# Decode rows of a hybrid layer spread over all 128 partitions, with the array used in four tiles

## The chip, the cores and the metric

One core of a Trainium2 chip runs one layer of a decoder trunk. The metric is the device time of one execution in microseconds. Of the engines, TensorE multiplies and transposes (PE in the profile, PEld its weight loads), VectorE (DVE) and ScalarE (ACT) work element by element and empty PSUM, GpSimd (POOL) prepares weight sums, and SyncE (SP) issues most transfers.

## The reference, cut to what matters

A layer mixes 1024 tokens of one prompt and 64 decode tokens (8 sequences of 8 tokens) with two groups of four heads of 128 columns, and then runs a convolutional feed-forward block. The retention heads work in chunks; the decode sequences are one chunk of 8 rows each with a state that is given:

```python
scores = jnp.einsum('bhnd,bhmd->bhnm', qc, kc) * dmat[None]
out = (jnp.einsum('bhnm,bhmv->bhnv', scores, vc)
       + jnp.einsum('bhnd,bhdv->bhnv', qc, S) * xi[None, :, :, None])
S_new = (S * chunk_decay[None, :, None, None]
         + jnp.einsum('bhmd,bhmv->bhdv', kc * zeta[None, :, :, None], vc))
```

Here `dmat` holds gamma to the power of the distance below the diagonal. An mLSTM head has the same three parts (own values, state, update) with weights `w` made of running gate sums, and a normaliser that rides along as a 129th column of the state. Each head's output is normalised per row and gated.

## The kernel before, in words

All tensors lie with features on partitions and tokens on columns: `q`, `k`, `v` of a head are 128 x 1088, 1024 prompt columns and then 64 decode columns. Projections run in split fp32 (three products per weight tile, `product`, L160) over four blocks of 272 columns.

`mix_head` handles one head. `front` (L571 on) takes one or two chunks of 128 columns, or the 64 decode columns as "chunk 8": it transposes k and v (L577, L578) into PSUM, scales k into `kz` and v into `vt`, for an mLSTM head broadcasts the gate rows over the partitions (L595, L597), adds the mask (L601) and takes the exponential (L603), then forms the scores (L618) and masks them into `pt` (L620). A retention head has a mask of its own with its decay in it, 128 columns for the prompt and 64 for the decode rows.

`pair_of` finishes two prompt chunks: update products (L706), own values (L711), the state product (L713), the state itself (L717, L719), and `stats`. `sample` finishes the decode rows, which lie on 64 partitions: q is laid out so that each sequence's 8 columns stand alone among 64 (`qx`, L665); one product of the own values (L667) and eight with the eight states (L669) add up in one PSUM tile of 64 rows. The values are then masked into eight copies, one for each sequence (`vx`, L674), and update products of three or four states each (L682) are added to the states on VectorE (L685 or L687). `finish` normalises rows, transposes them back (L655) and writes them to `yT` (L659, L661).

The order within a head is chunks 0 and 1, 2 and 3, the decode rows, 4 and 5, 6 and 7, each `front` written one step ahead, and each `finish` one step behind. The order of instructions on each engine is set by a planner, which follows the program's order as priority and a model of the times: it puts projection products of the next head between the small products. Small products and their results use six PSUM banks (`psB`), projections two (`psA`). GpSimd meanwhile prepares sums of feed-forward weights (L754).

Of the kernel before, what the change touches and what calls it, by code (L numbers as in the profile page):

```python
# [16 lines left out]
P = 128  # L17
D = 1024
KT = D // P
LP = 1024  # L20
# [25 lines left out]
C_ID, C_BLK, C_RM, C_RMS = 0, 128, 136, 136 + 512  # L46
C_ZE, C_XI, C_XI2 = C_RMS + 256, C_RMS + 264, C_RMS + 300
C_N = C_XI2 + 36
X_NEG, X_NEGS, X_SEL = 0, 128, 192
X_N = 192 + 1024  # L50


def _tables():
# [3 lines left out]
    s = np.arange(TS)  # L57
    up = i[:, None] <= i[None, :]
    same = s[:, None] // LS == s[None, :] // LS
    ups = same & (s[:, None] <= s[None, :])  # L60
    for h in range(NH):
        lg = LG[h]
        c[:, C_RM + h * P:C_RM + (h + 1) * P] = np.where(up, SCALE * np.exp(-(i[:, None] + 1) * lg), 0.0)
        c[:TS, C_RMS + h * TS:C_RMS + (h + 1) * TS] = np.where(
            ups, SCALE * np.exp(-(s[:, None] % LS + 1) * lg), 0.0)
        c[:, C_ZE + h] = SCALE * np.exp((CH - 1 - i) * lg)
        c[:TS, C_ZE + NH + h] = SCALE * np.exp((LS - 1 - s % LS) * lg)
        xi = np.ones((P, 9))
        xi[:, :8] = np.exp((i + 1) * lg)[:, None]
        xi[:TS, 8] = np.exp((s % LS + 1) * lg)  # L70
        c[:, C_XI + h * 9:C_XI + h * 9 + 9] = xi
        c[:, C_XI2 + h * 9:C_XI2 + h * 9 + 9] = xi * xi
    c[:TS, C_BLK:C_BLK + NB] = s[:, None] // LS == np.arange(NB)[None, :]
    x = np.zeros((P, X_N), np.float64)
    x[:, X_NEG:X_NEG + P] = np.where(up, 0.0, NEG)
    x[:, X_NEGS:X_NEGS + TS] = NEG
    x[:TS, X_NEGS:X_NEGS + TS] = np.where(ups, 0.0, NEG)
# [15 lines left out]
def hybrid_layer_kernel(ctx: ExitStack, tc: tile.TileContext, a: dict, o: dict):  # L93
# [211 lines left out]

    def token_norms():
        ps = bank(psB, 9, "rcol")
        for c in range(9):
            m = CH if c < 8 else TS
            nc.tensor.matmul(ps[:m, c:c + 1], rb[:, c * CH:c * CH + m], ident[:, 0:1], start=True, stop=True)  # L310
        nc.vector.tensor_copy(rcol[:, :8], ps[:, :8])
        nc.vector.tensor_copy(rcol[:TS, 8:9], ps[:TS, 8:9])
# [5 lines left out]
    negsb = mp.tile([P, TS], BF16, name="negsb")  # L318
# [28 lines left out]
    def gate_consts():  # L347
# [8 lines left out]
        nc.vector.tensor_copy(negsb, xst[:, X_NEGS:X_NEGS + TS])  # L356
# [16 lines left out]
    def gate_rows():  # L373
# [64 lines left out]
        for g in range(0, 9, 3):  # L438
            ps = bank(psB, 288, f"cols{g}").rearrange("p (i c) -> p i c", i=3)
            for i in range(3):  # L440
                c = g + i
                n = CH if c < 8 else TS
                nc.tensor.transpose(ps[:n, i, :68], stk[:, c * CH:c * CH + n], ident[:68, :68])
                nc.vector.tensor_copy(cols[:n, c, :].rearrange("p (j r) -> p j r", j=3),
                                      ps[:n, i, :].rearrange("p (j r) -> p j r", j=3)[:, :, :NH])
# [44 lines left out]

    def csl(c):
        return slice(c * CH, c * CH + (CH if c < 8 else TS))

    def rows_of(c):
        return CH if c < 8 else TS
# [29 lines left out]
    def mix_head(hd, ml):  # L525
# [44 lines left out]

        def front(cs):  # L571

            c0, L, n = cs[0], len(cs), rows_of(cs[0])
            nmc = f"{nm}{c0}"
            px = bank(psB, 512, f"x_{nmc}").rearrange("p (j i n) -> p j i n", j=2, i=2)
            for i, c in enumerate(cs):
                nc.tensor.transpose(px[:n, 0, i, :], k[:, csl(c)], ident)  # L577
                nc.tensor.transpose(px[:n, 1, i, :], v[:, csl(c)], ident)  # L578
            kz = m2.tile([P, 2, P], F32, tag="kz", name=f"kz_{nmc}")
            if ml:  # L580
                nc.vector.tensor_tensor(kz[:n, :L], px[:n, 0, :L, :],
                                        cols[:n, c0:c0 + L, NH + hd].unsqueeze(2).broadcast_to([n, L, P]), ALU.mult)
            else:
                zc = C_ZE + hd + (0 if c0 < 8 else NH)
                nc.vector.tensor_scalar(kz[:n, :L], px[:n, 0, :L, :], rc(zc, 1, n), None, ALU.mult)
            vt = vts[0]
            vts.append(vts.pop(0))
            for i, c in enumerate(cs):
                nc.scalar.activation(vt[:n, i, :P], px[:n, 1, i, :], AF.Copy, scale=rcol[:n, c:c + 1])
            qs = None  # L590
            if ml:
                pb = bank(psB, 512, f"w_{nmc}").rearrange("p (j i n) -> p j i n", j=2, i=2)
                cs_ = slice(c0 * CH, c0 * CH + L * n)
                flat2 = lambda j: pb[:, j].rearrange("p i n -> p (i n)")[:, :L * n]
                ins = nc.tensor.matmul(flat2(1), sel[:, 1, hd, :], uihl[:, cs_], start=True, stop=True)  # L595
                with tc.issue_after(ins.ins):
                    nc.tensor.matmul(flat2(0), sel[:, 0, hd, :], uihl[:, cs_], start=True, stop=False)  # L597
                wt, qs = (wq[:, turns["wq"] % 2, i].rearrange("p (i n) -> p i n", i=2) for i in range(2))
                turns["wq"] += 1
                for i, c in enumerate(cs):  # L600
                    nc.tensor.matmul(pb[:, 0, i, :n], idb, negb if c < 8 else negsb, start=False, stop=i == L - 1)  # L601
                for i, c in enumerate(cs):
                    nc.scalar.activation(wt[:n, i, :n], pb[:n, 0, i, :n], AF.Exp,  # L603
                                         bias=cols[:n, c, 2 * NH + hd:2 * NH + hd + 1])
                if c0 < 8:
                    nc.vector.tensor_copy(dec[:, c0:c0 + L], pb[:, 1, :, n - 1])
                else:
                    nc.vector.tensor_copy(dec[:, 8:16],
                                          flat2(1).rearrange("p (s l) -> p s l", s=NB)[:, :, LS - 1])
                qv = q[:, c0 * CH:c0 * CH + L * n].rearrange("p (i n) -> p i n", i=L)  # L610
# [827 lines left out]
```

## Time and profile before

| | us |
|---|---|
| median of 3 runs (1367.94 to 1368.15) | 1368.1 |
| span of the profiled execution | 1367.5 |
| that execution's time around its span, from the median | 0.6 |
| TensorE busy | 1345.5 |
| VectorE busy | 1005.6 |
| ScalarE busy | 594.3 |
| GpSimd busy | 428.2 |

The profile's times are microseconds from the start of the span. A matmul's length in it includes its way through the array, so neighbouring rows overlap; the difference of two starts is what an instruction costs. Rows that merge several instructions give the first start and the time to the last end. The retention heads run from 117 to 300 us, the mLSTM heads from 297 to 518 us.

### The profile page before, as it was taken

Reading aid. Unit: us, or ns where it says so; the run is one execution under the profiler, and the core shown is the slowest. Engines: PE = TensorE matmul, PEld = TensorE weight load, DVE = VectorE, ACT = ScalarE, POOL = GpSimd, SP = SyncE. Lnnn points to the kernel's source line nnn. Section 1 sums busy time; section 2 is a strip of 40 time slices with the busy share of each in tenths; the row PEclk is TensorE's granted clock in tenths of the full one; section 3 lists DMA queues with packets and bytes.
Section 4 is the critical chain, followed back from the end, with each engine's and each line's share of the span. In section 5 each row is a group of like instructions: output and inputs, shape, how many; then the busy total and the mean of one; then the engine's idle time right before and its main releaser. Section 6 shows DMA issues by size and latency. Waiting matters only on the chain.

```text
span 1367.5 us, 26897 instructions
## 1 busy us (share of the span) xinstructions
PE 1345.5 (98%) x10583; PEld 1321.4 (97%) x10583; DVE 1005.6 (74%) x2009; ACT 594.3 (43%) x1107; POOL 428.2 (31%) x565
## 2 busy tenths in 40 slices
PE   9999999999999999999989999999999999999996
PEld 9999999999999999999989999999999999999995
DVE  6878875556475366668799978778777788996667
ACT  7544333212222335546364434434334355454562
POOL 0354440579665000000143222221222205872002
PEclk9999999999999999999999999999999999999998
DMA  6434541477885111533124444443444359533363
GB/s 244 143 109 135 172 137 56 146 218 188 223 169 191 49 49 42 183 99 105 57 93 140 155 148 135 134 134 118 143 150 136 126 163 332 176 106 92 95 217 131
DMA packets 92734, 192.80 MB, mean 141 GB/s; under 512 B 16192, under 2 KB 41280, under 8 KB 92096
## 3 DMA queue, kind: packets, MB, share of 16 engines
q1 hardware_dynamic: 80304, 149.03, 33.3%
q0 software_dynamic: 12160, 41.95, 10.7%
q8 instruction: 83, 1.36, 0.4%
q14 instruction: 43, 0.35, 0.1%
q10 hardware_dynamic: 144, 0.11, 0.0%
HBM read 134.58 MB, written 56.47 MB: 140 GB/s over the span
## 4 chain that ended last, share of the span: by engine, by line
PE 92%; DVE 5%; issue 1%; ACT 1%; DMA 1%; SPq 0%; DVEq 0%
PE in L160 27%; PE out L160 6%; PE up_S L1046 6%; PE up_S L1044 6%; PE up_S L1045 6%; PE dn L1255 5%; PE dn L1257 5%; PE dn L1256 5%; PE up_A L1045 4%; PE up_A L1044 4%; PE up_A L1046 4%; PE up_A L1091 1%; PE up_A L1092 1%; PE up_A L1090 1%; PE s_m L618 1%
## 5 line engine op out<-in xcount | busy, mean ns | idle before, releaser
L160 PE MATMUL in<-hh,wh_in 128*128 128x272 f32 x1024 | 298.6, 294 | 1.5 <-ACT wh_in L144 1.5
L160 PE MATMUL in<-hh,wl_in 128*128 128x272 f32 x1024 | 296.4, 291 | 0.0
L160 PE MATMUL in<-hl,wh_in 128*128 128x272 f32 x1024 | 295.6, 291 | 0.0
L160 PEld LDWEIGHTS in<-hh,wh_in 128*128 128x128 f32 x1024 | 192.2, 188 | 4.6 <-issue 2.0
L160 PEld LDWEIGHTS in<-hh,wl_in 128*128 128x128 f32 x1024 | 192.4, 189 | 3.7 <-issue 3.5
L160 PEld LDWEIGHTS in<-hl,wh_in 128*128 128x128 f32 x1024 | 191.9, 188 | 1.7 <-issue 1.5
L144 ACT ACTIVATE wh_up<-st_up 128x1024 fp32r<-128x1024 f32 x84 | 80.4, 959 | 164.9 <-PE up_S L1045 100.5
L146 DVE TENSOR_TENSOR wl_up<-st_up,wh_up 128x1024 fp32r<-128x1024 f32 x84 | 96.5, 1151 | 9.3 <-ACT wh_up L144 9.3
L1184 DVE TENSOR_TENSOR rb<-rb 128x544 fp32r<-128x544 f32 x78 | 75.9, 979 | 36.5 <-ACT rb L1183 35.9
L1018 DVE TENSOR_TENSOR Uv<-Uv,up_S 128x272 f32<-128x272 f32 (+1 forms) x200 | 66.4, 376 | 45.5 <-PE up_S L1046 45.5
L754 POOL TENSOR_TENSOR tab<-tab 128x256 f32<-128x256 f32 x104 | 81.1, 790 | 13.7 <-DMA tab<-in_wu 9.3
L1183 ACT ACTIVATE rb<-rb 128x544 fp32r<-128x544 f32 x78 | 50.4, 650 | 77.1 <-DMA rb<-bd 61.8
L1204 POOL TENSOR_TENSOR wd<-wd 128x512 f32<-128x512 f32 x44 | 71.8, 1657 | 35.0 <-DMA wd<-in_wd 14.4
L1076 POOL TENSOR_TENSOR act<-act 128x544 f32<-128x544 f32 x40 | 64.7, 1618 | 55.2 <-DMA bd<-act 37.4
L1059 DVE SCALAR_TENSOR_TENSOR c<-Uv,vec,c 128x1024 f32<-128x1024 f32 (+1 forms) x88 | 69.0, 789 | 9.0 <-ACT c L1057 9.0
L1009 POOL MEMSET Ug<- 128x2 f32 x22 | 2.2, 99 | 227.7 <-DMA xr<-in_x 117.8
L1059 DVE SCALAR_TENSOR_TENSOR c<-Ug,vec,c 128x1024 f32<-128x1024 f32 x88 | 69.2, 825 | 0.6 <-ACT c L1057 0.6
L754 POOL TENSOR_TENSOR wq<-wq 128x256 f32<-128x256 f32 x56 | 51.0, 920 | 44.8 <-DMA wq<-in_wu 42.6
L754 POOL DMA_DIRECT2D tab<-in_wu x52 | 36.7, 713 | 67.4 <-DVE k_r L486 48.8
L1057 ACT ACTIVATE c<-Ug,vec 128x1024 f32<-128x1024 f32 (+1 forms) x44 | 34.6, 833 | 52.2 <-DVE Ug L1022 46.7
L1044 PE MATMUL up_S<-B3h,wh_up 128*128 128x272 f32 x160 | 47.4, 296 | 3.7 <-ACT Uv L1029 3.7
L146 DVE TENSOR_TENSOR wl_in<-st_in,wh_in 128x1024 fp32r<-128x1024 f32 (+2 forms) x33 | 40.8, 1236 | 13.3 <-ACT wh_in L144 13.3
(544 smaller groups left out, 4642.4 us busy)
## 6 DMA issues: line engine op xcount, KB each, us to landing
rb<-bd SPq DMA_DIRECT2D x76, 272.0 KB, 2.9
st_up<-sd SPq DMA_DIRECT2D x40, 512.0 KB, 3.9
bd<-act SPq DMA_DIRECT2D x33, 544.0 KB, 3.6
st_in<-in_wi SPq DMA_DIRECT2D x31, 512.0 KB, 4.2
tab<-in_wu POOLq DMA_DIRECT2D x52, 256.0 KB, 5.1
sd<-tab POOLq DMA_DIRECT2D x26, 512.0 KB, 3.6
st_up<-in_wu SPq DMA_DIRECT2D x24, 512.0 KB, 3.4
wd<-in_wd SPq DMA_DIRECT2D x44, 256.0 KB, 5.3
```

The source lines that it names most:

```text
L144: act = nc.scalar.activation(hi, x, AF.Copy)
L146: last["split"] = act, eng.tensor_tensor(lo, x, hi.bitcast(F32), ALU.subtract)
L160: nc.tensor.matmul(ps, u[:, k * P:(k + 1) * P], x[b // 2][k // 4][v][:, k % 4, qcols(b)], start=k == term == 0, stop=k == KT - 1 and term ...
L754: last["sums"] = f(*args)
L1044: nc.tensor.matmul(ps, wh[:, c], xh[:, k, n], start=k == 0, stop=False)
L1045: nc.tensor.matmul(ps, wh[:, c], xl[:, k, n], start=False, stop=False)
L1046: nc.tensor.matmul(ps, wl[:, c], xh[:, k, n], start=False, stop=k == 3)
L1059: nc.vector.scalar_tensor_tensor(c, u(i), cw(i), c, ALU.mult, ALU.add)
L1184: nc.vector.tensor_tensor(lo, x, hi.bitcast(F32), ALU.subtract)
L1204: nc.gpsimd.tensor_tensor(quad(p, out), quad(p, x), quad(p, y), op)
L1255: nc.tensor.matmul(t, wh[:, ms], ah, start=k == 0, stop=False)
L1256: nc.tensor.matmul(t, wh[:, ms], al, start=False, stop=False)
```

## The change

The 64 decode columns are spread: four groups of 32, of which the last 16 hold two sequences and the first 16 are the columns ahead of them (16 of the preceding data, masked out). So chunk 8 has 128 columns and its transposes 128 rows, like every other chunk. A view with overlapping windows gives q; k and v are copied by ScalarE into a tile of their own, since they are weights of the array. The state products write 32 partitions each, four groups side by side, and the updates contract 32 partitions each, four groups below one another. The eight masked copies of the values become two (first or second sequence of a group), and the updates four products of two states. The update products stand ahead of `stats`, in four banks taken together. The retention masks become one for the prompt and one for the decode rows; the head's decay comes in as a factor per row (`C_RS`) in a three-operand instruction. Tables and helpers follow (the tables' new layout is cut below).

```diff
+    c[:, C_RM:C_RM + P] = up
+    c[:, C_RMS:C_RMS + P] = ups
...
+        c[:, C_RS + h] = SCALE * np.exp(-(i + 1) * lg)
+        c[:, C_RS + NH + h] = SCALE * np.exp(-(s % LS + 1) * lg)
...
+    def chunk(t, c):
+
+        if c < NCH:
+            return t[:, c * CH:(c + 1) * CH]
+        v = t[:, LP - LEAD:]
+        return bass.AP(v.tensor, v.offset, [list(v.ap[0]), [TS // G, G], [1, GW]])
+
+    def spread(t):
+        return t.rearrange("p (g r) -> p g r", g=G)
+
+    def spread_copy(t, out):
+
+        nc.scalar.activation(spread(out), chunk(t, NCH), AF.Copy)
+        return out
+
+    def spread_tile(name):
+        return m2.tile([P, NB * 129], F32, tag="vx", bufs=1, name=name)
...
-    qx = mp.tile([P, NB * (TS + LS)], F32, name="qx")
+    qx = mp.tile([P, G, 2, GW + LS], F32, name="qx")
     nc.gpsimd.memset(qx, 0.0)
-    qown = qx.rearrange("p (s t) -> p s t", s=NB)[:, :, :LS]
+    qown = qx[:, :, :, LEAD:LEAD + LS]
+    qone = lambda g, e: qx[:, g].rearrange("p e r -> p (e r)")[:, GW * e:GW * (e + 1)]
...
+            if c0 < 8:
+                kc, vc = ([chunk(t, c) for c in cs] for t in (k, v))
+            else:
+                own.append(spread_tile(f"sp_{nm}"))
+                kc, vc = ([spread_copy(t, own[0][:, i * P:(i + 1) * P])] for i, t in enumerate((k, v)))
             for i, c in enumerate(cs):
-                nc.tensor.transpose(px[:n, 0, i, :], k[:, csl(c)], ident)
-                nc.tensor.transpose(px[:n, 1, i, :], v[:, csl(c)], ident)
+                nc.tensor.transpose(px[:, 0, i, :], kc[i], ident)
+                nc.tensor.transpose(px[:, 1, i, :], vc[i], ident)
...
             for i, c in enumerate(cs):
-                nc.tensor.matmul(ps[:, i, :], k[:, csl(c)], q[:, csl(c)], start=True, stop=True)
+                o_ = ps[:, i, :]
+                nc.tensor.matmul(o_ if c < 8 else spread(o_), kc[i], chunk(q, c), start=True, stop=True)
             pt = m2.tile([P, 2, P], F32, tag="pt", name=f"pt_{nmc}")
-            nc.vector.tensor_tensor(pt[:n, :L, :n], ps, mk, ALU.mult)
+            if ml:
+                nc.vector.tensor_tensor(pt[:, :L, :], ps, wt[:, :L, :], ALU.mult)
+            else:
+                m = rc(C_RM if c0 < 8 else C_RMS, P).unsqueeze(1).broadcast_to([P, L, P])
+                nc.vector.scalar_tensor_tensor(pt[:, :L, :], ps, rc(C_RS + hd + (0 if c0 < 8 else NH), 1), m,
+                                               ALU.mult, ALU.mult)
...
         def sample(kz, vt, qs, pt):
-            qv = qs[:, 0, :TS] if ml else q[:, LP:]
-            nc.vector.tensor_copy(qown, qv.rearrange("p (s l) -> p s l", s=NB))
-            po = bank(psB, W, f"o_{nm}8", rows=TS)
-            nc.tensor.matmul(po, pt[:TS, 0, :TS], vt[:TS, 0, :W], start=True, stop=False)
-            for i in range(NB):
-                nc.tensor.matmul(po, qx[:, i * TS:(i + 1) * TS], sb[:, i, :W], start=False, stop=i == NB - 1)
+            qv = spread(qs[:, 0, :])[:, :, LEAD:] if ml else spread(q[:, LP:])
+            nc.vector.tensor_copy(qown, qv.rearrange("p g (e t) -> p g e t", e=2))
+            po = bank(psB, W, f"o_{nm}8")
+            nc.tensor.matmul(po, pt[:, 0, :], vt[:, 0, :W], start=True, stop=False)
+            for e in range(2):
+                for g in range(G):
+                    nc.tensor.matmul(po[GW * g:GW * (g + 1), :], qone(g, e), sb[:, 2 * g + e, :W],
+                                     start=False, stop=e == 1)
...
-            stats(on, po.unsqueeze(1), 0, 1, TS, mv, f"{nm}s")
-            vx = m2.tile([TS, NB, 129], F32, tag="vx", bufs=1, name=f"vx_{nm}")[:, :, :W]
-            nc.vector.tensor_tensor(vx, vt[:TS, 0, :W].unsqueeze(1).broadcast_to([TS, NB, W]),
-                                    cst[:TS, C_BLK:C_BLK + NB].unsqueeze(2).broadcast_to([TS, NB, W]), ALU.mult)
+            vx = own[0][:, 2 * P:2 * P + 2 * W].rearrange("p (e v) -> p e v", e=2)
+            nc.vector.tensor_tensor(vx, vt[:, 0, :W].unsqueeze(1).broadcast_to([P, 2, W]),
+                                    cst[:, C_BLK:C_BLK + 2].unsqueeze(2).broadcast_to([P, 2, W]), ALU.mult)
+            ups = [bank(psB, 2 * W, f"us_{nm}{g}") for g in range(G)]
+            for g, up in enumerate(ups):
+                rows_ = slice(GW * g, GW * (g + 1))
+                nc.tensor.matmul(up, kz[rows_, 0, :], vx[rows_], start=True, stop=True)
+            stats(on, po.unsqueeze(1), 0, 1, mv, f"{nm}s")
             if ml:
                 nc.vector.tensor_tensor(sb, sb, dec[:, 8:16].unsqueeze(2).broadcast_to([P, NB, W]), ALU.mult)
-            step = 3 if ml else 4
-            for j in range(0, NB, step):
-                m = min(step, NB - j)
-                up = bank(psB, m * W, f"us_{nm}{j}").rearrange("p (s v) -> p s v", s=m)
-                nc.tensor.matmul(up, kz[:TS, 0, :], vx[:, j:j + m, :], start=True, stop=True)
-                sj = sb[:, j:j + m, :W]
+            for g, up in enumerate(ups):
+                up = up.rearrange("p (s v) -> p s v", s=2)
+                sj = sb[:, 2 * g:2 * g + 2, :W]
```

## Rows read from the trace of the kernel before

**Rows 1.** The page's first part: busy time, share of the span and instructions of each engine.

```profile
PE 1345.5 (98%) x10583; PEld 1321.4 (97%) x10583; DVE 1005.6 (74%) x2009; ACT 594.3 (43%) x1107; POOL 428.2 (31%) x565
```

**Rows 2.** The chain of waits that ended last, shares of the span by engine.

```profile
PE 92%; DVE 5%; issue 1%; ACT 1%; DMA 1%; SPq 0%; DVEq 0%
```

**Rows 3.** TensorE's waits between 50 and 540 us, the whole answer: engine, tile and line, who was waited for, us in total, times, longest.

```profile
PE yt_m L655 <- DVE on_m L653: 0.4, 1, 0.4
```

**Rows 4.** Busy time of each engine by stage: the last row of the answer, the sum over 120 to 510 us and the mean of its eight stretches, in us.

```profile
sum 390.00, PE 389.38 PEld 369.59 DVE 234.42 ACT 122.31 POOL 178.71; mean PE 48.67 PEld 46.20 DVE 29.30 ACT 15.29 POOL 22.34
```

**Rows 5.** TensorE's timeline over the decode rows of retention head 2: start us, length us, engine, line, operation, what it writes from what, rows and columns of the array, form, count of instructions merged.

```profile
219.82 0.61 PE L618 MATMUL s_r<-q_r,k_r 128*128 128x128 f32 x4
220.36 0.43 PE L667 MATMUL o_r<-vts,pt_r 64*64 64x128 f32 x2
220.72 1.97 PE L669 MATMUL o_r<-sb_r,qx 128*64 128x128 f32 x16
222.61 1.98 PE L682 MATMUL us_r<-vx_r,kz_r 64*128 64x512 f32 x4
224.52 0.39 PE L160 MATMUL in<-hh,wh_in 128*128 128x272 f32 x1
224.75 0.29 PE L160 MATMUL in<-hh,wl_in 128*128 128x272 f32 x1
224.88 0.28 PE L160 MATMUL in<-hl,wh_in 128*128 128x272 f32 x1
```

**Rows 6.** The same view from 222.28 us on, where the row takes only the last four instructions of L669.

```profile
222.08 0.60 PE L669 MATMUL o_r<-sb_r,qx 128*64 128x128 f32 x4
```

**Rows 7.** The weight loads of TensorE beside them.

```profile
220.71 1.73 PEld L669 LDWEIGHTS o_r<-sb_r,qx 128*64 128x64 f32 x16 [0.17 <-issue]
...
223.15 0.19 PEld L682 LDWEIGHTS us_r<-vx_r,kz_r 64*128 64x128 f32 x1 [0.24 <-issue]
223.58 0.19 PEld L682 LDWEIGHTS us_r<-vx_r,kz_r 64*128 64x128 f32 x1 [0.24 <-issue]
```

**Rows 8.** TensorE's timeline where the decode rows of the same head are transposed and scored (the scores, two instructions of L618, stand between the first two rows).

```profile
215.89 0.27 PE L578 MATMUL x_r<-cst,v_r 128*64 128x128 f32 x1
...
216.35 0.71 PE L706 MATMUL u_r<-vts,kz_r 128*128 128x128 f32 x4
216.90 0.39 PE L711 MATMUL o_r<-vts,pt_r 128*128 128x128 f32 x2
```

**Rows 9.** TensorE's timeline where the decode output of the same head is transposed.

```profile
230.50 0.39 PE L713 MATMUL o_r<-S_r,q_r 128*128 128x128 f32 x2
230.72 0.39 PE L711 MATMUL o_r<-vts,pt_r 128*128 128x128 f32 x2
231.04 0.27 PE L655 MATMUL yt_r2s<-cst,on_r2s 64*128 64x64 f32 x1
231.24 0.39 PE L160 MATMUL in<-hh,wl_in 128*128 128x272 f32 x1
231.47 0.29 PE L160 MATMUL in<-hl,wh_in 128*128 128x272 f32 x1
```

**Rows 10.** TensorE's timeline over the decode rows of mLSTM head 2.

```profile
433.57 0.43 PE L667 MATMUL o_m<-vts,pt_m 64*64 64x129 f32 x2
433.93 0.39 PE L160 MATMUL in<-hh,wh_in 128*128 128x272 f32 x1
434.16 0.38 PE L713 MATMUL o_m<-S_m,wq 128*128 128x129 f32 x2
434.47 1.99 PE L669 MATMUL o_m<-sb_m,qx 128*64 128x129 f32 x16
436.39 0.91 PE L682 MATMUL us_m<-vx_m,kz_m 64*128 64x387 f32 x2
437.23 0.39 PE L160 MATMUL in<-hh,wl_in 128*128 128x272 f32 x1
...
437.80 1.35 PE L682 MATMUL us_m<-vx_m,kz_m 64*128 64x387 f32 x4
439.08 0.39 PE L160 MATMUL in<-hh,wl_in 128*128 128x272 f32 x1
```

**Rows 11.** VectorE's normalising of the prompt chunks and TensorE's first transpose of them, in mLSTM heads 0 (two rows) and 2 (two rows).

```profile
332.40 3.17 DVE L653 TENSOR_SCALAR on_m<-on_m,mv_m,A_m 128x128 f32<-128x128 f32 x4
...
334.42 0.27 PE L655 MATMUL yt_m<-cst,on_m 128*128 128x128 f32 x1
...
441.02 1.12 DVE L653 TENSOR_SCALAR on_m<-on_m,mv_m,A_m 128x128 f32<-128x128 f32 x4
...
444.36 0.27 PE L655 MATMUL yt_m<-cst,on_m 128*128 128x128 f32 x1
```

**Rows 12.** Groups by form: line, engine, operation, what it writes from what, count: shortest/median/longest ns, first and last start, forms. The last row is a timeline row of ScalarE: the last piece of v of retention head 2.

```profile
L674 DVE TENSOR_TENSOR vx_r<-vts,cst x4: 1209/1210/1514, 132.0 to 269.1; 64x1024 f32<-64x1024 f32 x4
...
L687 DVE SCALAR_TENSOR_TENSOR sb_r<-sb_r,us_r x8: 660/688/690, 140.2 to 276.8; 128x512 f32<-128x512 f32 x8
...
L620 DVE TENSOR_TENSOR pt_r<-s_r,tab x20: 205/410/425, 121.1 to 282.1; 128x256 f32<-128x256 f32 x16, 64x64 f32<-64x64 f32 x4
...
L624 ACT ACTIVATE on_r2s<-o_r x1: 270/270/270, 222.7 to 222.7; 64x128 f32<-64x128 f32 x1
...
210.88 0.40 ACT L471 ACTIVATE v_r<-in 128x272 f32<-128x272 f32 x1 [2.61 <-PE in L160]
```

More of the change, by code (lines that the diff above doesn't have):

```diff
@@ L304, in pre_norm @@
             nc.vector.tensor_tensor(rot[i][:, o0:o0 + n], rot[i][:, o0:o0 + n], rb[:, o0:o0 + n], ALU.mult)
+    def chunk(t, c):
[10 more added lines that the diff above has]
+        return m2.tile([P, NB * 129], F32, tag="vx", bufs=1, name=name)
     def token_norms():
         ps = bank(psB, 9, "rcol")
+        rs = spread_copy(rb, spread_tile("sp_rb")[:, :P])
         for c in range(9):
[L309 to L312, printed above, removed]
+            nc.tensor.matmul(ps[:, c:c + 1], chunk(rb, c) if c < 8 else rs, ident[:, 0:1], start=True, stop=True)
+        nc.vector.tensor_copy(rcol, ps)
     idb = mp.tile([P, P], BF16, name="idb")
@@ L441, in gate_rows @@
                 c = g + i
[L442 to L445, printed above, removed]
+                x = chunk(stk, c) if c < 8 else spread_copy(stk, spread_tile("sp_stk")[:68, :P])
+                nc.tensor.transpose(ps[:, i, :68], x, ident[:68, :68])
+                nc.vector.tensor_copy(cols[:, c, :].rearrange("p (j r) -> p j r", j=3),
+                                      ps[:, i, :].rearrange("p (j r) -> p j r", j=3)[:, :, :NH])
     yT = []
@@ L489, in evac_rot @@
         return f
[L491 to L495, printed above, removed]
     def early_gate(hid):
@@ L616, in front @@
-            ps = bank(psB, 2 * P, f"s_{nmc}").rearrange("p (i n) -> p i n", i=2)[:n, :L, :n]
-            for i, c in enumerate(cs):
-                nc.tensor.matmul(ps[:, i, :], k[:, csl(c)], q[:, csl(c)], start=True, stop=True)
-            pt = m2.tile([P, 2, P], F32, tag="pt", name=f"pt_{nmc}")
-            nc.vector.tensor_tensor(pt[:n, :L, :n], ps, mk, ALU.mult)
+                    nc.vector.tensor_copy(dec[:, c0:c0 + L], pb[:, 1, :, P - 1])
+                    qv = q[:, c0 * CH:(c0 + L) * CH].rearrange("p (i n) -> p i n", i=L)
@@ L635, in finish @@
+            small = lambda tag: m2.tile([P, 4], F32, tag=tag, name=f"{tag}_{name}")[:, :L]
             vv, A = small("vv"), small("A")
@@ L650, in finish @@
             nc.vector.tensor_tensor(A, A, rd, ALU.mult)
-            ps = bank(psB, L * n, f"yt_{name}")
+            ps = bank(psB, L * P, f"yt_{name}")
             for i in range(L):
-                nc.vector.tensor_scalar(on[:n, i, :P], on[:n, i, :P], mv[:n, i, 0:1], A[:, i:i + 1],
+                nc.vector.tensor_scalar(on[:, i, :P], on[:, i, :P], mv[:, i, 0:1], A[:, i:i + 1],
                                         ALU.subtract, ALU.mult)
-                nc.tensor.transpose(ps[:, i * n:(i + 1) * n], on[:n, i, :P], ident[:n, :n])
-            y = yT[hid // 2][:, hid % 2, c0 * CH:c0 * CH + L * n]
+                nc.tensor.transpose(ps[:, i * P:(i + 1) * P], on[:, i, :P], ident)
+            y = yT[hid // 2][:, hid % 2, c0 * CH:c0 * CH + L * P if c0 < 8 else T]
+            if c0 == 8:
+                ps, y = spread(ps)[:, :, LEAD:], spread(y)
             gain = vec[:, V_HEAD + hid:V_HEAD + hid + 1]
@@ L712, in pair_of @@
                     if c:
-                        prev = nc.tensor.matmul(po[:, i, :], qs[:, i, :] if ml else q[:, csl(c)], S,
+                        prev = nc.tensor.matmul(po[:, i, :], qs[:, i, :] if ml else chunk(q, c), S,
                                                 start=False, stop=True)
```

98 lines of the change are left out of this document (49 added, 49 removed).

## The prediction

> **What bounds the kernel now.** I read the page's busy shares first, then the chain of waits, then what TensorE waited for in the stage that the change touches, then that stage instruction by instruction. TensorE is busy for 98% of the span and the chain that ended last is TensorE for 92% [rows 1, 2]. Busy time alone says little, since its matmuls overlap. The stronger sign is the list of TensorE's waits from 50 to 540 us, all of the projections and heads: one wait, 0.4 us [rows 3]. The planner fills every gap of a head with projection matmuls of the next one, which follow each other every 0.125 us [rows 5]. In 390 us of that stage VectorE works 234 us and ScalarE 122 us [rows 4]. So a microsecond of TensorE issue time taken out of a head is a microsecond of the span, as long as nothing that TensorE waits for is just in time. The other engines' changes count only there.
>
> **What TensorE pays today for the decode rows of one head.** I take retention head 2, where nothing else lies between. An fp32 matmul stands in the trace as two matmul instructions with a weight load each. Full-array instructions over 128 columns follow each other every 0.11 us: two of them fill 230.50 to 230.72 [rows 9]. The own scores end at 219.82 + 4 x 0.11 = 220.26. The projection is back in step at 224.75 - 0.125 = 224.63 [rows 5]. That is 4.37 us for the product with the own values (L667), eight state products (L669) and two updates (L682).
>
> Changing the shape of the array costs extra there. The last four instructions of L669 begin at 222.08, so the next of that kind would begin at 222.52; L682 begins at 222.61, 0.09 later [rows 6]. Then the first instruction of the new shape has its weight load uncovered: L682's first step is 223.15 - 222.61 = 0.54 where the next is 223.58 - 223.15 = 0.43 [rows 6, 7], and the first projection step after it is 0.23 where 0.125 is usual [rows 5]. So a change costs 0.09 plus 0.11 with 128 weight columns. For 32 columns I estimate 0.03, a quarter of 0.11.
>
> **The change, part by part, on TensorE.**
> *Outputs and updates.* After it the own product is full shape (2 x 0.11 = 0.22); then into column tiles (0.09 + 0.03), 16 instructions over 128 columns (X), into row tiles (0.09 + 0.11), 8 instructions over 256 columns (Y), and out (0.09 + 0.11): 0.74 + X + Y. A 256-column step is half of 0.43, 0.215. The trace of before holds no two tiles side by side, so X and Y are bounded. Without any overlap X = 16 x 0.11 = 1.76 and Y = 8 x 0.215 = 1.72: 4.22 us, 0.15 saved. With all four tiles abreast X is four steps and three weight loads (0.53) and Y two steps and three loads (0.43 + 0.11): 1.81 us, 2.56 saved. I take a value between. The code issues tile after tile, and a tile's two instructions follow each other; the second must wait for its own first, and what is queued behind it waits too, if matmuls begin in order. Then only the second of one tile overlaps the first of the next: X = 9 x 0.11 = 0.99, Y = 5 x 0.215 = 1.08: 2.81 us, 1.56 saved.
>
> The Trainium skill (TensorE: Matmul & The Clock Gate, "The mechanism") says that a weight load overlaps a running matmul only if the row group differs; column tiles share all rows, which would speak against X. In L669 the 16 weight loads already lie beside the matmuls of the same rows, at steps of 0.11 (16 in 1.73 us) [rows 7], so the trace does not bear it out; by the rule X would be above 1.76 and the updates alone would gain.
>
> *Shapes that go.* The decode scores were 64 columns wide: from the transpose at 215.89 to the product at 216.90 is 1.01 us; in full shape it is 0.11 + 2 x 0.11 + 4 x 0.11 = 0.77, with the doubled columns in it: 0.24 saved [rows 8]. The transpose of the decode output had 64 rows: 230.72 to 231.47 is 0.75; in full shape 0.22 + 0.11 + 0.125 = 0.46: 0.29 saved [rows 9]. The mLSTM row broadcasts and mask gain 64 columns each, at most 3 x 0.03 = 0.09 per head; I leave it out. So a retention head saves 1.56 + 0.53 = 2.1 us (0.7 to 3.1).
>
> *mLSTM heads.* In head 2 the same work runs from 433.48 (0.09 before L667) to 439.08 + 0.105, 5.7 us, with four projection instructions (0.5) and L713 (0.22) in between: 4.98, since the work there is cut and each cut pays two changes of shape [rows 10]. Against 2.81 that is 2.17 + 0.53 = 2.7; one cut that stays costs 0.4, so I take 2.4 for heads 2 and 3 (1.3 without overlap).
>
> In heads 0 and 1 a wait takes over. VectorE normalises the four prompt chunks from 332.40 to 335.57 and TensorE's transposes of them begin at 334.42, in the middle of it; in head 2 they end at 442.14 and are read from 444.36 [rows 11]. An earlier TensorE only waits there, while what VectorE does before (scaling and adding the states) moves up by what the outputs gain, 0.77 and a little. I take 1.0 each (0 to 2.4).
>
> Sum: 4 x 2.1 + 2 x 2.4 + 2 x 1.0 = 15.2 us.
>
> **What costs nothing.** *ScalarE*: two copies per head that put k and v of the decode rows in place, by the nearest row 0.27 us each [rows 12]. The last piece of v is written by 210.88 + 0.40 and the transpose of v reads it at 215.89 [rows 8, 12], 4.6 us later; without that cover they cost 0.55 x 8 = 4.4 us. *VectorE*: the masked values shrink from 1.21 us to about 0.4 (258 columns instead of 1032). The state updates become four of 256 columns: 4 x 0.35 (half of 0.69) to 4 x 0.41, against 2 x 0.69 [rows 12]. The common mask needs a multiply by a column too, between 0 and 0.28 more (0.41 to 0.69) for each of 16 products, 4.5 us at most; VectorE idles 156 us of this stage [rows 4]. Loads: a shorter constant table, off TensorE's path.
>
> The profiled execution spans 1367.5 us, the median of the runs is 1368.1; 0.6 lies around the span and stays. 1367.5 - 15.2 + 0.6 = 1352.9, so 1353.
>
> **Rivals.**
> *All four tiles abreast.* The weight loads run ahead and the two instructions of a tile don't hold up the next: 4 x 3.1 + 2 x 3.7 + 2 x 1.2 = 22 us, 1346. For it: weight loads already run beside the matmul before them [rows 7]. Against: 128-column loads take 0.11 of a load path each, eight of them 0.88, more than two 0.215 steps. The Trainium skill states this course in a fact of its own (TensorE: Matmul & The Clock Gate, "Measured speedup vs the span model"): tiles start about 4 ns apart, and four row tiles measured 3.07x.
>
> *The tiles don't run at once.* The change doesn't do what its name says; only the shapes that go are gained: 4 x 0.68 + 2 x 1.3 + 2 x 0.5 = 6.3, 1362. For it: nothing in this trace shows two tiles together.
>
> *Slower: the tile groups are cut.* Each update needs a bank of its own, four beside the output's, out of six. Where they are not free at once the planner puts projection work between the tiles, as it does between the updates of head 2 at 437.23 [rows 10]. Each cut is two changes of shape, 0.09 + 0.105 and 0.09 + 0.11, 0.4 us. With no overlap two cuts per head eat the gain; with the forecast's overlap it takes five. Four cuts a head without overlap: 32 x 0.4 - 6.3 = +6.5, 1375. Against: the 16 state products stayed together [rows 5, 10].
>
> **How the numbers follow.** Forecast 0.5 (its own range 1349 to 1357), abreast 0.15, not at once 0.23, cut 0.08, and 0.04 for a gain eaten to nothing, by waits like that of heads 0 and 1 in all heads. From no change (1368) the measurement tells 0.2%, 2.7 us. Faster 0.88, same 0.04, slower 0.08. The range 1343 to 1365 leaves out the cut, the eaten gain and the far end of abreast.
>
> **What would show it.** In the changed trace the state products' instructions of different tiles should begin closer than 0.11 us, nine steps per head in 1.0 us; steps of 0.11 throughout would mean no overlap, and four to five of them all four abreast. The updates' steps should add to 1.1 us. No extra step of 0.09 should stand at the decode scores and the output transposes. In mLSTM heads 0 and 1 TensorE's waits for L653's counterpart should grow to a microsecond or more; if they don't, the gain is larger. The prediction is wrong if VectorE's or ScalarE's new work appears as a wait of TensorE in the other heads, or if projection instructions stand between the tiles.

## The result and the profile after

The changed kernel takes 1352.2 us (median of four runs, 1349.2 to 1354.3), the kernel before on the same chip 1368.1: a ratio of 0.9878, 95% interval [0.9862, 0.9894]. Its profiled execution spans 1351.1 us, 16.4 less than before, and took 1353.2, so 2.1 lie around the span. Lines have moved: L160 is now L164, the own values L698, the state products L701, the updates L711, the scores L643, the transposes of the output L684, VectorE's normalising L682.

The page of the changed kernel, busy times (as [rows 1]) and the chain of waits (as [rows 2]):

```profile
PE 1328.3 (98%) x10607; PEld 1310.2 (97%) x10607; DVE 1001.9 (74%) x2020; ACT 595.6 (44%) x1125; POOL 432.5 (32%) x565
...
PE 85%; DVE 9%; ACT 3%; DMA 2%; issue 2%; DVEq 0%; SPq 0%; ACTq 0%
```

TensorE lost 17.2 us of busy time and is still the engine that bounds. Where it went is seen at the last projection product, which began at 540.9 us before and at 523.4 now (the last number but the forms in this line view, first and last start):

```profile
L164 PE MATMUL in<-hl,wh_in x1024: 282/289/394, 7.7 to 523.4; 128*128 128x272 f32 x171
```

So 17.5 us come from the stage that the change touches. What follows it takes 1.2 us more (827.7 against 826.5); in a second run of the changed kernel (after_again, below) it takes 826.2, so this is the scatter between runs. TensorE's waits from 50 to 545 us, the whole answer (as [rows 3]):

```profile
PE out L164 <- DVE z L531: 1.0, 1, 1.0
PE yt_r L684 <- DVE on_r L682: 0.6, 1, 0.6
PE out L164 <- DVE wol L150: 0.3, 1, 0.3
PE yt_m L684 <- DVE on_m L682: 0.2, 1, 0.2
```

The first stands behind the last projection, which lay past the window of [rows 3]; the others are tenths of a microsecond. The decode rows of retention head 2 in TensorE's timeline (as [rows 5]; start, length, line, what from what, rows*columns, count):

```profile
219.78 0.39 PE L698 MATMUL o_r<-vts,pt_r 128*128 128x128 f32 x2
220.10 0.65 PE L701 MATMUL o_r<-sb_r,qx 128*32 128x128 f32 x16
220.68 0.70 PE L711 MATMUL us_r<-sp_r,kz_r 32*128 32x256 f32 x4
221.31 0.39 PE L164 MATMUL in<-hh,wh_in 128*128 128x272 f32 x1
221.54 0.28 PE L164 MATMUL in<-hh,wl_in 128*128 128x272 f32 x1
...
222.25 0.69 PE L711 MATMUL us_r<-sp_r,kz_r 32*128 32x256 f32 x2
222.88 0.39 PE L164 MATMUL in<-hh,wh_in 128*128 128x272 f32 x1
...
223.45 0.69 PE L711 MATMUL us_r<-sp_r,kz_r 32*128 32x256 f32 x2
224.07 0.39 PE L164 MATMUL in<-hh,wh_in 128*128 128x272 f32 x1
```

Two things are to be seen. The sixteen state products take 220.68 - 220.10 = 0.58 us with the change of shape behind them, where before they took 1.89 [rows 5]. The same view in windows that end at 220.13, 220.26 and 220.37, and one that begins at 220.67, shows how:

```profile
220.10 0.32 PE L701 MATMUL o_r<-sb_r,qx 128*32 128x128 f32 x4
...
220.10 0.43 PE L701 MATMUL o_r<-sb_r,qx 128*32 128x128 f32 x8
...
220.10 0.54 PE L701 MATMUL o_r<-sb_r,qx 128*32 128x128 f32 x12
...
220.45 0.30 PE L701 MATMUL o_r<-sb_r,qx 128*32 128x128 f32 x4
```

They begin in four batches of four; in a batch the starts lie some 0.007 us apart, and the next batch begins 0.11 to 0.13 later.

The updates are not in one piece. Two tiles go at 220.68, the third and the fourth alone at 222.25 and 223.45, with projections between them. Each piece takes about 0.63 us from its start to the next instruction's, whether it has four instructions (two tiles) or two (one tile), and each pays two changes of shape: the last step ahead of it and the first projection step after it are 0.21 and 0.23 instead of 0.125. In mLSTM head 2 one tile goes alone and three together, the three in the same time:

```profile
422.26 0.65 PE L701 MATMUL o_m<-sb_m,qx 128*32 128x129 f32 x16
422.84 0.70 PE L711 MATMUL us_m<-sp_m,kz_m 32*128 32x258 f32 x2
423.46 0.39 PE L164 MATMUL in<-hh,wh_in 128*128 128x272 f32 x1
...
425.28 0.71 PE L711 MATMUL us_m<-sp_m,kz_m 32*128 32x258 f32 x6
425.92 0.40 PE L164 MATMUL in<-hh,wl_in 128*128 128x272 f32 x1
```

Over the eight heads that is 4, 3, 3, 3, 2, 2, 2 and 2 pieces, 21 in all.

To add this up I took, for each TensorE instruction, the time from its start to the next one's start, and for the instructions next to the state products and updates what goes beyond their usual step (the changes of shape). State products and updates together, us per head:

| | r0 | r1 | r2 | r3 | m0 | m1 | m2 | m3 | sum |
|---|---|---|---|---|---|---|---|---|---|
| before | 4.28 | 4.01 | 3.93 | 3.93 | 4.44 | 4.43 | 4.43 | 4.43 | 33.9 |
| after | 3.81 | 3.05 | 3.05 | 3.05 | 2.25 | 2.24 | 2.25 | 2.25 | 22.0 |

The own product, in full shape now, gives another 0.14 per head (0.36 to 0.22): 11.9 + 1.1 = 13.0 us. By the same steps the shapes that went gave 4.5: scores 16.9 to 15.8, transposes of k and v 15.9 to 14.9, prompt update products 14.8 to 13.6, transposes of the output 6.2 to 5.0. The scores hold the 0.09 us that entering the own product cost before (0.7 in all). Together 17.5, what the last projection shows.

### The profile page after: what moved, and what is told of

It is laid out like the page before. It is cut to its first block, busy times and chain, and to the rows that moved or that the text cites. A ratio compares the mean times of both kernels' runs of the same rounds, so it can differ in the third digit from the quotient of the medians.

```text
span 1351.1 us, 26966 instructions
## 1 busy us (share of the span) xinstructions
PE 1328.3 (98%) x10607; PEld 1310.2 (97%) x10607; DVE 1001.9 (74%) x2020; ACT 595.6 (44%) x1125; POOL 432.5 (32%) x565
## 4 chain that ended last, share of the span: by engine, by line
PE 85%; DVE 9%; ACT 3%; DMA 2%; issue 2%; DVEq 0%; SPq 0%; ACTq 0%
PE in L164 23%; PE up_S L1080 6%; PE up_S L1078 6%; PE up_S L1079 6%; PE out L164 5%; PE up_A L1079 4%; PE up_A L1078 4%; PE up_A L1080 4%; PE dn L1289 4%; PE dn L1290 4%; PE dn L1291 4%; PE up_A L1125 1%; PE up_A L1126 1%; PE up_A L1124 1%; DMA rb<-bd 1%
## 5 line engine op out<-in xcount | busy, mean ns | idle before, releaser
L164 PE MATMUL in<-hh,wh_in 128*128 128x272 f32 x1024 | 298.8, 294 | 1.3 <-ACT wh_in L148 1.3
L164 PE MATMUL in<-hh,wl_in 128*128 128x272 f32 x1024 | 296.9, 292 | 0.0
L164 PE MATMUL in<-hl,wh_in 128*128 128x272 f32 x1024 | 296.0, 291 | 0.0
L164 PEld LDWEIGHTS in<-hh,wh_in 128*128 128x128 f32 x1024 | 192.3, 188 | 5.6 <-issue 3.3
L164 PEld LDWEIGHTS in<-hh,wl_in 128*128 128x128 f32 x1024 | 192.4, 189 | 2.6 <-issue 2.3
L164 PEld LDWEIGHTS in<-hl,wh_in 128*128 128x128 f32 x1024 | 192.0, 188 | 1.3 <-issue 1.0
L788 POOL TENSOR_TENSOR tab<-tab 128x256 f32<-128x256 f32 x104 | 82.1, 800 | 16.9 <-DMA tab<-in_wu 12.5
```

The lines of the kernel that those rows point to most:

```text
L164: nc.tensor.matmul(ps, u[:, k * P:(k + 1) * P], x[b // 2][k // 4][v][:, k % 4, qcols(b)], start=k == term == 0, stop=k == KT - 1 and term ...
L788: last["sums"] = f(*args)
```

## The experiments

The theory at this point: the column tiles run abreast and give more than forecast; the row tiles run abreast too, but the cuts (projection instructions between the tiles, which break the group into pieces) give their gain back, at 0.63 + 0.09 + 0.1 = 0.82 us for each piece. The rivals: the shapes alone are the gain, or a kernel with fewer pieces would turn the gain into waits. The first four ran on one chip beside the kernel before (1369.8 us), the next four beside it too (1369.1), the last three too (1368.6).

**after_again**: the changed kernel, unaltered.

> The changed kernel itself, on the same chip as the next three. It should lie near 1352 us, ratio 0.988 to the kernel before, by every theory; it is the base for the other three.

Measured: 1350.5 us, ratio 0.9863 [0.9849, 0.9878]. It is the base for what follows.

**held**: the updates wait until the decode statistics are under way, so that four banks should be free together.

```diff
+            stats(on, po.unsqueeze(1), 0, 1, mv, f"{nm}s")
-            nc.vector.tensor_tensor(vx, ...)
+            with tc.issue_after(last["bn"].ins):
+                nc.vector.tensor_tensor(vx, ...)
...
-            stats(on, po.unsqueeze(1), 0, 1, mv, f"{nm}s")
```

> The masked values are formed on VectorE only after the statistics of the decode output, so that four banks are free when the first update product can start, and the planner places the four products of each of the eight heads in one piece: 8 pieces where the changed kernel has 21. Theory 1 (a cut piece costs its own two steps and two changes of shape, 0.62 + 0.09 + 0.11 = 0.82 us in the trace of the changed kernel, whether it holds one tile or three): 13 pieces fewer give 13 x 0.82 = 10.7 us, near 1341.5. Rival 2 (row tiles side by side gain nothing, only the changes of shape go): 13 x 0.4 = 5.2 us, 1347. Rival 3 (the later updates make TensorE wait for VectorE instead): 1350 or above, with several us of TensorE's waits between 50 and 530 us, where the changed kernel has 1.8.

Measured: 1346.9 us (1343.6 to 1351.2), 0.9838 [0.9812, 0.9864]. Each head has one piece, and state products and updates fall to 1.62 us per head, 13.0 in all: 9.0 less than in the changed kernel. The last projection began only 1.8 us earlier (521.6). TensorE's waits from 50 to 545 us, the whole answer:

```profile
PE in L164 <- DVE k_r L508: 2.5, 1, 2.5
PE yt_m L684 <- DVE on_m L682: 1.1, 3, 0.7
PE out L164 <- DVE z L531: 1.0, 1, 1.0
PE yt_r L684 <- DVE on_r L682: 0.6, 2, 0.3
PE w_m L622 <- DVE sb_m L720: 0.5, 1, 0.5
PE x_r L600 <- DVE sb_r L722: 0.2, 1, 0.2
```

The time is that of the second rival, but its reason is not: the issue time fell as the first theory says, and waits took much of it back. The largest was followed up below.

**cols_only**: column tiles kept, updates back on the whole array over eight masked copies.

```diff
-            ups = [bank(psB, 2 * W, f"us_{nm}{g}") for g in range(G)]
...
+            for j in range(0, NB, step):
...
+                nc.tensor.matmul(up, kz[:, 0, :], vx[:, j:j + m, :], start=True, stop=True)
```

> The column tiles stay, the updates go back to full-array products over eight masked copies (128 rows, 512 or 387 and 258 columns). Theory 1 (the row tiles are cut so often that they gain nothing): the 21 pieces of the changed kernel cost 21 x 0.82 = 17.2 us, full-array products cost 4 x 0.43 plus one change of 0.2 per head, 15.4 us; so 1350 to 1351, a little faster than the changed kernel. Rival (the row tiles bring what the prediction's sum has for them, 1.72 - 1.08 = 0.64 us per head): 5 us slower than the changed kernel, 1357.

Measured: 1351.5 us, 0.9868 [0.9853, 0.9883], within 1 us of after_again. As cut by the planner, the row tiles gain nothing. In head 2 the four instructions of a whole-array update need no second change of shape: the projection's row begins early, at 220.30, beside the last of them, and the next one begins at 220.83, so the update takes 220.83 - 0.125 - 218.88 = 1.82 us, a first step of 0.53 and three of 0.43. By the steps, state products and updates add to 20.6 us there, against 22.0.

```profile
218.31 0.65 PE L701 MATMUL o_r<-sb_r,qx 128*32 128x128 f32 x16
218.88 1.98 PE L715 MATMUL us_r<-sp_r,kz_r 128*128 128x512 f32 x4
220.30 0.69 PE L164 MATMUL in<-hh,wl_in 128*128 128x272 f32 x1
220.83 0.29 PE L164 MATMUL in<-hl,wh_in 128*128 128x272 f32 x1
```

**tile_by_tile**: the four instructions of one column tile behind each other, then the next tile's.

```diff
-            for e in range(2):
-                for g in range(G):
+            for g in range(G):
+                for e in range(2):
```

> The eight state products are issued with the two of one tile next to each other instead of the four tiles in turn; the planner also cuts the updates into 24 pieces instead of 21, worth 3 x 0.82 = 2.5 us. Theory 1 (matmuls begin in the order of the program, and only neighbours of different tiles overlap): the 16 instructions take 13 steps of 0.11 where they now take 4, 1.0 us more per head, 8 us, so 1352 + 8 + 2.5 = near 1362. Rival (each tile takes its own instructions as they come, whatever lies between): still 4 steps, and only the 2.5 us, near 1354.5.

Measured: 1353.2 us, 0.9884 [0.9868, 0.9901]. The sixteen state products still take 0.60 us in head 2, and the batches of four are still there, now 0.013 us apart within one (the second row is that of a window that ends at 219.16):

```profile
219.10 0.67 PE L701 MATMUL o_r<-sb_r,qx 128*32 128x128 f32 x16
...
219.10 0.34 PE L701 MATMUL o_r<-sb_r,qx 128*32 128x128 f32 x4
```

So a tile's queue does not hold up the next tile's. The distance fits that: the next tile's first instruction is now four places behind in the program, where it was two, and starts 0.013 us later instead of 0.007. The 2.7 us above after_again are the updates: the new order made 24 pieces of them, and state products and updates add to 24.6 us against 22.0.

**held_act**: as held, but ScalarE masks the values, behind its copy of the decode output, so that VectorE has no masking to do and the updates don't wait for its statistics.

```diff
-            nc.vector.tensor_tensor(vx, ...)
+            with tc.issue_after(last["copied"].ins):
+                for e in range(2):
+                    nc.scalar.activation(vx[:, e, :], vt[:, 0, :W], AF.Copy, scale=cst[:, C_BLK + e:C_BLK + e + 1])
```

> As in the run with the updates held together, but the two masked copies of the values are made on ScalarE, right behind its copy of the decode output, instead of on VectorE behind the statistics. The planner again places the four update products of each head in one piece. Theory (in the held run TensorE lost 5 us to waits for VectorE, of which the changed kernel has none at the same places: 2.7 us at the k of the next head, the rest at the transposes of the normalised output, because the masked values and all that follows them stood late in VectorE's queue): with that work off VectorE the waits between 50 and 545 us shrink from 8.3 us to about 3 and the kernel comes to 1342 or 1343. Rival (the waits come from the states being ready later, whoever makes the copies): they stay, 1347.

Measured: 1341.7 us (1339.7 to 1343.9), 0.9799 [0.9786, 0.9813], the fastest of all. Eight pieces of eight instructions, 0.65 us each, in head 2:

```profile
215.14 0.65 PE L701 MATMUL o_r<-sb_r,qx 128*32 128x128 f32 x16
...
219.20 0.71 PE L713 MATMUL us_r<-sp_r,kz_r 32*128 32x256 f32 x8
219.85 0.39 PE L164 MATMUL in<-hh,wh_in 128*128 128x272 f32 x1
```

State products and updates add to 12.9 us, as in held, and the waits from 50 to 545 us are two:

```profile
PE out L164 <- DVE z L531: 1.0, 1, 1.0
PE yt_m L684 <- DVE on_m L682: 0.5, 2, 0.2
```

The last projection begins at 513.7, 9.7 us earlier than in the changed kernel: 9.0 from the pieces, the rest from small steps.

**held_ret**: held in the retention heads only.

> The updates are held together on VectorE in the four retention heads alone (9 of the 13 pieces fewer); the mLSTM heads stay as in the changed kernel. By the price of a piece 9 x 0.82 = 7.4 us less issue time, against waits that the held run showed in the retention heads, 4.2 us at 144, 155 and 274 us: near 1347.5. If the waits of the mLSTM heads (2.8 us in the held run) ate all that their 4 pieces gave, this run equals the held run; if they did not, it is about 1 us slower.

Measured: 1346.9 us, 0.9836 [0.9822, 0.9849]. Its profile has the 2.5 us wait of held too (2.4 in the list of waits), and lacks held's steps of 0.3 to 0.9 us between 325 and 381 us, 2.7 in all. One piece in an mLSTM head saves 0.63 (2.25 to 1.62), 2.5 in four: in held the mLSTM heads' waits ate what their pieces gave. That the two medians are equal adds little to it, since the runs of held lie in two groups (below).

**no_factor**: `nc.vector.tensor_tensor(pt[:, :L, :], ps, m, ALU.mult)` in place of the three-operand product. **two_copies**: `for _ in range(2):` around ScalarE's copy of k and v.

> The changed kernel with the retention mask alone: the per-row factor of the decay is left out of the product with the mask (retention outputs lack it), so VectorE runs a two-operand instruction there as before the change. Theory (the three-operand instruction costs VectorE at most 16 x 0.28 us and TensorE nothing): the same time within 1.5 us, near 1350.5 to 1352. Rival (VectorE's longer instruction is on the path in the retention heads): 3 us faster.

> The changed kernel with every ScalarE copy of decode rows made twice: two more per head (k and v) and two more in all, 0.3 us each. Theory (the copies lie ahead of the transposes that need them by several us): no change within 1.5 us. Rival (TensorE waits for them): 8 x 0.6 = 4.8 us slower, 1356.

Measured: 1349.7 us, 0.9858 [0.9844, 0.9871], and 1350.8 us, 0.9867 [0.9853, 0.988]. Neither differs from after_again by more than the intervals: the factor costs nothing that can be measured (no_factor has 20 pieces instead of 21, which alone is worth its 0.8 us), and the copies are covered with room for as many again.

**held_again, held_sel, after_sel**: what the wait of 2.5 us in held is. In held ScalarE's timeline before that wait reads (the bracket: idle before it, and what ended that):

```profile
151.19 0.37 ACT L654 ACTIVATE on_r<-o_r 128x256 f32<-128x256 f32 x1
155.37 1.06 ACT L379 ACTIVATE sel<-xsel 100x1024 fp32r<-100x1024 f32 x1 [3.81 <-DMA xsel<-in_cx]
156.33 0.36 ACT L654 ACTIVATE on_r<-o_r 128x256 f32<-128x256 f32 x1
```

and VectorE's in the same place:

```profile
156.73 0.49 DVE L657 BATCH_NORM_STATS2 bn_r<-on_r 128x6 f32<-128x128 f32 x2 [3.78 <-ACT on_r L654]
...
157.75 0.44 DVE L508 TENSOR_TENSOR k_r<-in,tab 128x272 f32<-128x272 f32 x1
```

The selection table `xsel` is loaded into the buffer that the states of head 0 leave (tag `sb`), once these are stored; its conversion stands at the head of ScalarE's queue, behind it the copy of the prompt outputs, behind that VectorE's statistics, and behind those `k_r`, which frees a projection bank. VectorE, which the list of waits names, had itself waited. held_sel and after_sel move the conversion off ScalarE:

```diff
-        nc.scalar.activation(sel, xsel[:100, :].rearrange(...), AF.Copy)
+        nc.gpsimd.tensor_copy(sel, xsel[:100, :].rearrange(...))
```

> The kernel held once more, beside the next two on one chip. Its runs lay far apart (1343.6 to 1351.2 us), those of held_act did not (1339.7 to 1343.9). If its TensorE wait of 2.5 us at 155 us is a transfer that lands late (the load of the selection table, for which ScalarE's conversion L379 stands at the head of its queue for 3.8 us), the wait differs from run to run: 0 to 3 us, and the time is again 1343 to 1351. If it is VectorE's own load, the wait is 2.5 us again within some tenths.

> held with the conversion of the selection table (L379, 1.06 us, which waits for its load) moved from ScalarE to GpSimd, so that nothing stands behind it on ScalarE. Theory A: the 2.5 us wait of TensorE at 155 us is that load's, through ScalarE's queue (the copy of the outputs, L654), VectorE's queue (L657, then k_r L508) and a projection bank; it goes, and the time is 2 to 3 us below held_again's, 1343.5 to 1345. Theory B: VectorE is the bound there, behind the statistics that the updates now wait for; the wait stays at 2 us or more and the time at held_again's within 1 us.

> The changed kernel with the same move of L379 to GpSimd. There TensorE has no wait at 155 us, so the move alone should be worth nothing: 1350 to 1351.5 us. If it gives 2 us or more here too, then a gain of held_sel says nothing of held's wait.

Measured: held_again 1344.3 us (1343.7 to 1351.0), 0.9835 [0.9816, 0.9853], with no wait at 155 us in its profile: the conversion began at 151.59 there. Of the nine runs of held and held_again six lie from 1343.6 to 1345.0 and three from 1348.9 to 1351.2. held's profiled run (1348.9 us) is of the three and shows the wait, held_again's (1343.8) is of the six and doesn't. So the wait is an event of some runs and no fixed load of VectorE's; that the other late runs have the same cause is inferred from their times.

Two things belong to it that the list of waits doesn't show. The conversion is 3.8 us later in held than in held_again, and only half of that is the transfers': the states' store was issued 1.9 us later (145.41 against 143.52), the store and the load behind it took 1.0 and 0.9 us more. The store was late because VectorE finished the states late: three of its instructions took 0.5 us longer each, of which two are shown (held, then held_again). All three ran beside GpSimd's weight sums (140.24 to 144.49). In held_again the sums lay at 140.82 to 145.23, and one instruction was longer there, by 0.5 us. That the meeting of the two engines is the reason is argued from such rows; no run moved the sums.

```profile
140.34 0.93 DVE L509 TENSOR_TENSOR sw_qr<-sw_qr,tab 128x272 f32<-128x272 f32 x1
142.93 0.97 DVE L510 TENSOR_TENSOR q_r<-q_r,sw_qr 128x272 f32<-128x272 f32 x1
...
140.01 0.43 DVE L509 TENSOR_TENSOR sw_qr<-sw_qr,tab 128x272 f32<-128x272 f32 x1
141.57 0.43 DVE L510 TENSOR_TENSOR q_r<-q_r,sw_qr 128x272 f32<-128x272 f32 x1
```

And the wait costs more than its 2.5 us. TensorE stood until 158.25, and from 159.6 to 163.0 its granted clock was 0.5 of full speed, the lower of its two levels (1.2 of 2.4 GHz); a projection step takes 0.227 us there instead of 0.125. Held lags held_again by 0.4 us before the wait, by 3.1 behind it and by 4.3 at the end of that stretch, which is most of the 5.2 us between the two spans. The row has the stretch, TensorE's busy time and instructions, the granted clock and the DMA's share and GB/s:

```profile
159.60:163.00 3.40, 3.40 (x18) 0.50 0.74 214
```

held_sel took 1350.7 us, 0.9882 [0.9866, 0.9899]. Its profiled run (1355.0 us) has no wait at 155 us, but held_again's has none either, so this decides nothing between the two theories. The median is 6.4 us above held_again's: GpSimd came to the conversion at 168.7 us, behind its weight sums, the buffer came free for the states of head 1 only then, and TensorE waited for these, with a granted clock of 0.5 from 170 to 180 us behind it:

```profile
PE o_r L701 <- DMA sb_r<-in_sr: 8.2, 1, 8.2
```

So the path of the wait is read from the order of the queues in held, and no run shows what its removal is worth. after_sel (0.9906 [0.988, 0.9932]; five runs from 1350.0 to 1361.0 with a median of 1356.4, and one at 1851.6 apart from all others) scatters too far to serve as the control that it was meant to be; I draw nothing from it.

## Why the prediction was right, and where it was not

**The time and the mechanism.** 1353 was forecast and 1352.2 measured; TensorE's issue time in the decode rows was the place, and 15.2 us of it was the sum against 16.4 in the span. The single terms were less good, and that their errors cancel is luck. (The 0.6 us that the sum adds around the span compares one execution's span with the median of others. In the runs that have both, 1.7 to 2.2 us lie between an execution's time and its own span, so that term is not shown; by the medians the gain is 15.9 us.) By the table above, with the own product, the outputs and updates gave 3.7 us in the four retention heads (forecast 4 x 1.56 = 6.2), 4.6 in mLSTM heads 2 and 3 (forecast 2 x 1.87 = 3.7) and 4.7 in heads 0 and 1 (forecast 0.9 without the shapes). The shapes gave 4.5 (forecast 8 x 0.53 = 4.2), and 1.2 were lost behind the projections. -2.5 + 0.9 + 3.8 + 0.3 - 1.2 = 1.3, within rounding the distance of the two sums.

**State products.** The step that failed is "the second must wait for its own first, and what is queued behind it waits too, if matmuls begin in order". The first half holds: a lone update tile's second instruction comes 0.32 us after its first. The second half falls: with two tiles queued one behind the other, the starts come in pairs (a step has as many instructions as the piece has tiles; the rows don't name the tile), and tile_by_tile leaves the time of the state products as it was. So X was 0.46 us (0.58 less the 0.09 of the change and the 0.03 of the first load, which the sum has by themselves), not 0.99, and even under the 0.53 that stood as its lower bound. The rival "all four abreast" was right in this term. The Trainium skill (TensorE: Matmul & The Clock Gate, "Measured speedup vs the span model") has tiles starting about 4 ns apart; here it is 7, and the sixteen products went from 1.89 to 0.58 us, 3.3 times less. The rule on row groups that the Trainium skill states there ("The mechanism"), and that I weighed, does not hold for these column tiles either: they share all rows, and sixteen loads and products go in four steps.

**Updates.** Here the rival of the cut groups was right in its mechanism, together with the one of tiles abreast. I forecast Y at 1.08 in one piece. A whole group of four in one piece takes 0.65 (held_act). That holds 0.11 of the first weight load and 0.09 of the change out of the shape, which the sum has by themselves, so Y was 0.45, two steps of 0.215 and hardly more. The lower bound of 0.54 named three loads and counted 0.11 for them, one load's; and the objection that eight loads of 0.11 are more than two steps falls, since the four tiles' loads run beside each other. In held_act (a window that ends at 219.25) four begin within 0.02 us and take as long as one [rows 7]:

```profile
219.20 0.20 PEld L713 LDWEIGHTS us_r<-sp_r,kz_r 32*128 32x128 f32 x4
```

But the planner made 21 pieces, each as long as the whole group. The price of a cut was put at 0.4 us, its two changes of shape. It is 0.82, since a piece with fewer tiles is no shorter: it has its two steps of 0.215 as well, 0.43 + 0.4. A lone tile's 0.63 us are then 0.11 for the first load, 0.43 for two steps and 0.09 for the change out of the shape. The last update of mLSTM head 2 in the kernel before, with 258 columns and no tile beside it, goes at the same pace, 0.22 to the row below and 0.305 from there to the projection at 439.08 [rows 10]:

```profile
438.78 0.38 PE L682 MATMUL us_m<-vx_m,kz_m 64*128 64x258 f32 x1
```

Thirteen needless pieces at 0.82 are 10.7 us; held_act has them back, less what its state products pay for standing alone (out of the column tiles and into the row tiles, 8 x 0.2): 9.1 by this working, 9.0 by the sums over the heads. The diff's four banks "taken together" did not keep the group together; the planner put projections between, as [rows 10] had shown for the kernel before. That it was waiting for the later banks is argued from held and held_act, where every group is whole; no run gave the kernel more banks.

**Heads 0 and 1.** "A wait takes over" failed. In the changed kernel VectorE normalises the four chunks of head 0 in 1.12 us, where [rows 11] had 3.17 us for the same four (the first row is from after, the second from before):

```profile
328.21 1.12 DVE L682 TENSOR_SCALAR on_m<-on_m,mv_m,A_m 128x128 f32<-128x128 f32 x4
...
332.43 3.05 POOL L754 TENSOR_TENSOR tab<-tab 128x256 f32<-128x256 f32 x4
```

Before, no other work of VectorE's stood between the four either. Each took 0.76 to 0.89 us instead of 0.34 while GpSimd made four of its weight sums at the same time, and each ended 0.1 us after one of them did. In the changed kernel GpSimd makes none between 328.2 and 329.3. So the 3.17 us were a meeting of two engines, and no bound for a kernel in which they meet elsewhere. The wait named in the prediction appears as 0.2 us.

**What costs nothing** held on all points: two_copies for ScalarE, no_factor for the common mask, and no new wait of VectorE's longer than 0.6 us. The masked values fell from 1.21 to 0.42 us and the state updates are 16 of 0.41, as estimated from [rows 12]:

```profile
L706 DVE TENSOR_TENSOR sp_r<-vts,cst x4: 415/422/585, 132.3 to 265.6; 128x256 f32<-128x256 f32 x4
...
L721 DVE SCALAR_TENSOR_TENSOR sb_r<-sb_r,us_r x16: 403/414/425, 139.0 to 273.3; 128x256 f32<-128x256 f32 x16
```

**The signs that were named.** "Projection instructions stand between the tiles" was given as a sign that the prediction is wrong; they do stand there, and the time came out as forecast. With the tiles of each head together the kernel takes 1342 (held_act, where ScalarE also masks the values). The total alone would have hidden both errors.

What stays open: the working of a piece's 0.63 us is read from rows, since no run changed the number of columns of an update; and how often VectorE's instructions meet GpSimd's sums, and what that costs in all, was not tried.

## What to carry to other kernels

Tiles of the array pay only while their instructions stand together: count the pieces in the trace, and price each at the steps of a whole group plus two changes of shape. Where a planner cuts a group because its output banks come free one by one, let the group wait for an event behind which all banks are free, and let an engine with slack produce the operand that it waits for. A wait that the list puts down to one engine is worth following through that engine's own queue: here it led, three queues back, to a transfer into a shared buffer, and from there to VectorE again, at work beside GpSimd. Look at the granted clock behind a wait too, since a slow stretch there is part of its price.

## What the runs showed of the hardware

The four tiles of the array do not keep one common order of starts: instructions queued behind a tile's second instruction began before it, in column tiles (state products in four batches, 0.58 and 0.60 us for the two orders in which they were written) and in row tiles (two, three or four tiles in 0.63 to 0.65 us, where one takes 0.63). The weight loads of four row tiles ran beside each other (four in 0.20 us). The tiles' gain is lost by cutting, not by the order of the instructions within a group.

Some of VectorE's instructions took longer while GpSimd summed: four of 0.34 us took 0.76 to 0.89 each in mLSTM head 0 of the kernel before, two of 0.43 took 0.93 and 0.97 in held. Others beside the sums kept their length, and no run moved the sums away, so this is seen side by side and not by experiment.
